# The first stage of a hybrid attention block: channel factors in 128-column steps on GpSimd, squares summed by halves and by TensorE, roots for two row tiles at a time

## The chip, the cores and the metric

The kernel runs on one core of one Trainium2 chip. The metric is the device time of one execution in microseconds (us), as the median of repeated runs. The engines are called by the letters of the profile: PE is TensorE (matmuls; PEld its weight loads), DVE is VectorE, ACT is ScalarE, POOL is GpSimd and SP is SyncE, which here only issues DMAs.

## The reference, cut to what matters

One block of a language model: a normalised projection, two mixers (a sparse attention and a gated linear attention), an output projection, and a convolutional feed-forward part. The change lies in the first two lines of the block alone, the normalisation and the part of the projection that makes the attention's keys and values, its gate logits and the low-rank gate input of the linear attention.

```python
def rms_norm(x, g):
    xf = x.astype(jnp.float32)
    y = xf * lax.rsqrt(jnp.mean(xf * xf, axis=-1, keepdims=True) + EPS)
    return (y * g.astype(jnp.float32)).astype(x.dtype)
...
    for l in range(DEPTH):
        z = rms_norm(h, attn_norm[l]) @ w_in[l]
        nq, nkv, ngate, gq, gk, gv, glr, gout = jnp.split(z, offs, axis=-1)
        o_nsa = nsa_mixer(...)
        o_gla = gla_mixer(...)
        h = h + jnp.concatenate([o_nsa, o_gla], axis=-1) @ w_out[l]
        u = causal_dwconv(rms_norm(h, ffn_norm[l]) @ w_up[l], conv_w[l], conv_b[l])
        gate, up = jnp.split(u, 2, axis=-1)
        h = h + (jax.nn.silu(gate) * up) @ w_down[l]
```

There are 1024 rows of 1024 channels, all in float32.

## The kernel before, in words

A float32 matrix product is made of three matmuls in the type fp32r: each operand is split into a high part (ACT copies it into fp32r, line L57) and a low part (an engine subtracts the high part from the original, line L60), and `zmm` adds high x high (L118), high x low weight (L119) and low x high weight (L120) for each of the 8 blocks k of 128 channels.

The first stage walks over 8 row tiles t of 128 rows. For each tile, `x_first` loads the transposed x as `xraw` (128 channels x 8 blocks k x 128 rows, 512 KB), squares it on ACT into `xsq` (L252), multiplies it in place by the channel factors `again` (L253: on DVE for t = 0, on POOL after that, one instruction of 1024 columns), and splits it in two halves `xt` (ACT L57, DVE L60). `x_stat` sums the squares over the 8 blocks k with one DVE reduction (L264, read with a stride), over the 128 partitions with a matmul against a column of ones (L265, written by the profile as two passes), and takes the inverse square root `rx` of that one column by twelve small DVE steps (`rsqrt`, L66 to L73 for one column; with more than one column the three Newton steps use the other form, L75 to L77).

The tile then goes through two products: with `WA` (296 columns: the inputs of the two compressions, and 40 columns of gates) and with `WC` (512 columns: selected and window keys and values). The row factor `rx` is applied when the results leave PSUM: two DVE instructions for WA (`kcvc` L289, `gl` L290), one on ACT (L201) and one on DVE (L204) for WC. `zp` gives two PSUM banks for these products, so a third product waits until one has been emptied. Then come norms and rotations of the keys, eight transposes (L220), and the split `xt` goes to memory (`x_d`, L294) for the later products. `x_first` and `x_stat` run two tiles ahead of the products.

The weights WA are loaded in four pairs of blocks k (`araw`, 303 KB each) and split with the low part on DVE and POOL in turn; the eight blocks of WC (`wraw`, four buffers) in the same way.

After the first stage come the two compressions, the query product, the attention with the linear attention woven into it (to about 600 us), and then the output projection and the feed-forward part. The order of the instructions on each engine is not the order of the program text: the framework's scheduler plans the whole kernel with a simulated timeline and a priority, and what it plans is fixed in the queue of each engine.

```python
    with tile.TileContext(nc, schedule_with_timeline_sim=True) as tc:
        body(tc, aps, o)
```

## Time and profile before

| what | value |
|---|---|
| median of 3 runs | 1359.92 us (1358.54 to 1360.41) |
| the profiled execution, its own time | 1360.02 us |
| span of the program in the profile | 1357.8 us |
| PE busy | 1311.7 us (97%) |
| PE weight loads busy | 1094.1 us (81%) |
| DVE busy | 1087.3 us (80%) |
| ACT busy | 701.8 us (52%) |
| POOL busy | 285.2 us (21%) |

The profiled execution took 2.2 us more than the span that its profile covers, which is the time before the first and after the last instruction. Busy shares are averages over the whole span. A matmul's duration in the trace includes the time in the pipeline, so that consecutive matmuls overlap; what a stream of them costs is read from the distance between their starts.

### The profile page before, as it was taken

To read this page: it belongs to the slowest core of one execution; us is meant where nothing else is said; L and a number is where in the kernel's file an instruction comes from. 1 tells how busy PE (TensorE), PEld (TensorE's weight loads), DVE (VectorE), ACT (ScalarE), POOL (GpSimd) and SP (SyncE) were. 2 spreads that over 40 slices of the span, in tenths; PEclk is the share of its full clock that TensorE was granted. 3 is DMA by queue.
4 is the path that set the end of the run, shared out by engine and by line. 5 is a ranking of instruction groups with operands and counts; after the bars stand their busy time and mean duration, and the time that the engine had idled before them with its cause. 6 is when DMAs were issued, how large, how long until landed. Compare 5 with 4: busy or idle time off the path is not lost.

```text
span 1357.8 us, 19773 instructions
## 1 busy us (share of the span) xinstructions
PE 1311.7 (97%) x6618; PEld 1094.1 (81%) x6618; DVE 1087.3 (80%) x2584; ACT 701.8 (52%) x1383; POOL 285.2 (21%) x437
## 2 busy tenths in 40 slices
PE   6899999999999998999999999999999998999998
PEld 5788788888888886768788888888888886888887
DVE  7996866788797869971688998888788878699774
ACT  5343666678665666663454544444444444444431
POOL 4222124549344455432500000000000000000000
PEclk9999999999999999999999999999999998999999
DMA  8537673325222224112742132222222229664173
GB/s 303 204 119 269 218 241 93 107 79 171 81 91 65 83 84 121 35 40 84 249 140 95 62 106 81 79 79 92 94 78 78 78 84 350 238 204 155 34 232 122
DMA packets 80535, 177.07 MB, mean 130 GB/s; under 512 B 10785, under 2 KB 22962, under 8 KB 80434
## 3 DMA queue, kind: packets, MB, share of 16 engines
q1 hardware_dynamic: 54450, 111.84, 24.7%
q0 software_dynamic: 10368, 37.75, 9.2%
q10 hardware_dynamic: 15616, 26.22, 5.3%
q8 instruction: 52, 0.85, 0.2%
q14 instruction: 49, 0.40, 0.1%
HBM read 133.84 MB, written 41.94 MB: 129 GB/s over the span
## 4 chain that ended last, share of the span: by engine, by line
PE 80%; DVE 12%; DMA 2%; issue 2%; ACT 2%; POOL 0%; SPq 0%; ACTq 0%; DVEq 0%; POOLq 0%
PE pda L982 9%; PE pdb L982 7%; PE z L118 4%; PE z L120 4%; PE z L119 4%; PE O L466 4%; PE S L448 4%; PE pt L459 3%; PE uZ L679 3%; PE uX L680 3%; PE uX L679 3%; PE uX L681 3%; PE uZ L680 3%; PE uZ L681 3%; PE uW L681 3%; PE uW L680 3%
## 5 line engine op out<-in xcount | busy, mean ns | idle before, releaser
L118 PE MATMUL z<-whi,xt 128*128 128x512 f32 (+1 forms) x384 | 141.7, 369 | 4.6 <-DVE rx L68 2.3
L119 PE MATMUL z<-wlo,xt 128*128 128x512 f32 (+1 forms) x384 | 140.3, 365 | 0.3 <-DVE wlo L60 0.2
L120 PE MATMUL z<-whi,xt 128*128 128x512 f32 (+1 forms) x384 | 139.8, 364 | 0.0
L60 DVE TENSOR_TENSOR PTl<-pt,PTh 128x512 fp32r<-128x512 f32 (+1 forms) x148 | 100.5, 684 | 35.1 <-ACT PTh L57 33.8
L453 ACT ACTIVATE P<-P,m 128x640 f32<-128x640 f32 (+7 forms) x128 | 94.0, 736 | 57.3 <-DVE m L450 55.0
L57 ACT ACTIVATE PTh<-pt 128x512 fp32r<-128x512 f32 (+1 forms) x148 | 86.2, 593 | 53.3 <-PE pt L459 44.8
L527 POOL TENSOR_SCALAR P<-P,sc 128x640 f32<-128x640 f32 (+7 forms) x128 | 89.6, 711 | 76.0 <-DVE sc L473 38.3
L448 PE MATMUL S<-kst,qst 128*128 128x320 f32 (+5 forms) x384 | 99.7, 352 | 4.1 <-DVE m L450 3.3
L57 ACT ACTIVATE wuh<-wuraw 128x512 fp32r<-128x512 f32 x65 | 40.6, 631 | 103.8 <-PE uZ L680 52.8
L459 PE MATMUL pt<-ident,P 128*128 128x128 f32 x528 | 85.4, 273 | 0.9 <-DVE PTl L60 0.8
L118 PEld LDWEIGHTS z<-whi,xt 128*128 128x128 f32 x384 | 73.7, 192 | 14.8 <-issue 2.5
L119 PEld LDWEIGHTS z<-wlo,xt 128*128 128x128 f32 x384 | 73.5, 191 | 10.3 <-DVE wlo L60 0.7
L120 PEld LDWEIGHTS z<-whi,xt 128*128 128x128 f32 x384 | 73.5, 191 | 10.1 <-issue 0.2
L57 ACT ACTIVATE wuh<-ws 128x512 fp32r<-128x512 f32 x76 | 47.6, 632 | 64.3 <-PE uW L680 30.1
L57 ACT ACTIVATE dh<-g 128x1024 fp32r<-128x1024 f32 x44 | 46.7, 1064 | 65.9 <-PE pdb L982 24.3
L459 PEld LDWEIGHTS pt<-ident,P 128*128 128x128 f32 x528 | 65.9, 140 | 15.5 <-PE S L448 1.4
L448 PEld LDWEIGHTS S<-kst,qst 128*128 128x128 f32 x384 | 63.4, 191 | 16.0 <-DVE m L450 9.3
L982 PE MATMUL pda<-dl,dh 128*128 128x512 f32 x176 | 68.3, 389 | 0.0
L982 PE MATMUL pda<-dh 128*128 128x512 f32 x176 | 68.3, 389 | 0.0
L982 PE MATMUL pda<-dh,dl 128*128 128x512 f32 x176 | 68.3, 389 | 0.0
L792 ACT ACTIVATE y<-u,cb,cw 128x1024 f32<-128x1024 f32 x44 | 54.4, 1240 | 20.3 <-DVE u L871 14.6
L466 PE MATMUL O<-PTl,Vst 128*128 128x512 f32 x132 | 58.6, 444 | 6.2 <-DVE PTl L60 6.0
(473 smaller groups left out, 3899.1 us busy)
## 6 DMA issues: line engine op xcount, KB each, us to landing
xt<-x_d POOLq DMA_DIRECT2D x48, 512.0 KB, 3.7
wuraw<-in_wU_dram SPq DMA_DIRECT2D x42, 512.0 KB, 3.7
dv<-in_wD_dram SPq DMA_DIRECT2D x55, 256.0 KB, 3.3
act_d<-y SPq DMA_DIRECT2D x22, 512.0 KB, 2.7
dv<-act_d SPq DMA_DIRECT2D x44, 256.0 KB, 3.5
x_d<-xt ACTq DMA_DIRECT2D x16, 512.0 KB, 4.7
xt<-mix_d POOLq DMA_DIRECT2D x16, 512.0 KB, 4.2
g<-in_wD_dram SPq DMA_DIRECT2D x22, 256.0 KB, 5.6
```

The costliest lines, as they stand in the source:

```text
L57: A.activation(dst, src, AF.Copy, scale=scale)
L60: (eng or V).tensor_sub(dst, src, hi.bitcast(F))
L118: T.matmul(ps, x[:, 0], wh, start=(k == 0), stop=False)
L119: T.matmul(ps, x[:, 0], wl, start=False, stop=False)
L120: T.matmul(ps, x[:, 1], wh, start=False, stop=(k == NK - 1))
L448: T.matmul(ps[:, :e - c], qst[:, h], kcols(i, c, e), start=(i == 0), stop=(i == 1))
L453: A.activation(Pt, Pt, AF.Exp, bias=m, scale=-1.0, accum_out=sc)
L459: T.transpose(tp[:n, h], get(h), ident)
L466: T.matmul(O, Vt, y[:n], start=(nmm[0] == 0), stop=(nmm[0] == total - 1))
L680: T.matmul(ps, wh[:, k], bl[:, k], start=False, stop=False, skip_group_check=True)
L681: T.matmul(ps, wl[:, k], bh[:, k], start=False, stop=(k == 3 and last), skip_group_check=True)
L982: T.matmul(ps[t], l[:, ts], r, start=(j == 0 and n == 0 and not add), stop=(j == NH - 1 and n == 2), skip_group_check=True)
```

## The change

`x_first` no longer squares. For tile 0 it loads x in two halves, with the first weight slices between them, and DVE multiplies each half by the factors; for the other tiles POOL does it in eight instructions, one for each block k, of 128 columns with the factor as a per-partition scalar. The product goes to a tile of its own, `xg` (one buffer). `x_stat` squares `xraw` in place on ACT, adds its halves twice on DVE (512 columns, then 256), and TensorE sums the two blocks that are left with two matmuls whose weights are the squares. Even and odd tiles share one PSUM tile, and the root is taken for two columns at once after the odd tile. The first four blocks of WA come one by one through the buffers of `wraw`, the other four in two pairs, and every low part of WA and WC is now made by DVE. Tile 1's x is loaded and its root taken ahead of the loads of WC. `kcvc` and `gl` become views of one tile `kg`, written by one instruction.

```diff
-        kcvc = cc.tile([128, NT, 256], F, name="kcvc")
-        gl = cc.tile([128, NT, 40], F, name="gl")
+        kg = cc.tile([128, NT, NA], F, name="kg")
+        kcvc, gl = kg[:, :, :256], kg[:, :, 256:]
...
-            def x_first(t, eng):
+            def x_first(t):
                 raw = xr_p.tile([128, NK, 128], F, name="xraw")
-                SY.dma_start(raw, I["xT"][t])
-                sq = xr_p.tile([128, NK, 128], F, name="xsq", bufs=1)
-                A.activation(sq, raw, AF.Square)
-                eng.tensor_tensor(raw, raw, again[:, :, None].to_broadcast([128, NK, 128]), op=OP.mult)
+                halves = [slice(4 * i, 4 * i + 4) for i in range(2)]
+                for i, ks in enumerate(halves if t == 0 else [slice(0, NK)]):
+                    SY.dma_start(raw[:, ks], I["xT"][t, :, ks])
+                    if t == 0:
+                        wa_load(2 * i)
+                        wa_load(2 * i + 1)
+                xg = xr_p.tile([128, NK, 128], F, name="xg", bufs=1)
                 xt = []
-                for i in range(2):
+                for i, ks in enumerate(halves):
+                    if t == 0:
+                        V.tensor_tensor(xg[:, ks], raw[:, ks], again[:, ks, None].to_broadcast([128, 4, 128]), op=OP.mult)
+                    else:
+                        for k in range(4 * i, 4 * i + 4):
+                            P.tensor_scalar(xg[:, k], raw[:, k], again[:, k:k + 1], 1.0, op0=OP.mult, op1=OP.mult)
                     x = (xfp if i else xtp).tile([128, 2, 4, 128], R, name="xt")
-                    split(x[:, 0], x[:, 1], raw[:, 4 * i:4 * i + 4], V)
+                    split(x[:, 0], x[:, 1], xg[:, ks], V)
                     xt.append(x)
-                return xt, sq
-
-            def x_stat(t, sq):
-                st = pp.tile([128, 512], F, name="st", tag="h1", bufs=2)
-                ssq = c2.tile([128, 128], F, name="ssq", tag="vv")
-                V.tensor_reduce(ssq, sq.rearrange("p k t -> p t k"), axis=X, op=OP.add)
-                T.matmul(st[:, 0:1], ssq, ones, start=True, stop=True)
-                rsqrt(c2, rx[:, t:t + 1], st[:, 0:1], 1.0 / D, 1)
...
+            def x_stat(t, raw, kept=[]):
+                if t % 2 == 0:
+                    kept.append(pp.tile([128, 512], F, name="st", tag="h1", bufs=2))
+                st, c = kept[-1], t % 2
+                A.activation(raw, raw, AF.Square)
+                for n in (4, 2):
+                    V.tensor_tensor(raw[:, 0:n], raw[:, 0:n], raw[:, n:2 * n], op=OP.add)
+                for k in range(2):
+                    T.matmul(st[:, c:c + 1], raw[:, k], ones, start=(k == 0), stop=(k == 1), skip_group_check=True)
+                if c:
+                    rsqrt(c2, rx[:, t - 1:t + 1], st[:, 0:2], 1.0 / D, 2)
...
+            def wa_load(k):
+                if k < 4:
+                    wa_raw[k] = rawp.tile([128, 512], F, name="wraw")[:, :NA]
+                    SY.dma_start(wa_raw[k], I["wA"][k // 2, :, k % 2])
+                else:
+                    wa_raw[k] = wap.tile([128, 2, NA], F, name="araw", bufs=2)
+                    SY.dma_start(wa_raw[k], I["wA"][k // 2])
+            SY.dma_start(again, I["again"])
+            xts[0], sq = x_first(0)
+            for k in (0, 1, 2, 3, 4, 6):
+                if k > 3:
+                    wa_load(k)
+                    split(wah[:, k:k + 2], wal[:, k:k + 2], wa_raw[k], V)
+                else:
+                    split(wah[:, k], wal[:, k], wa_raw[k], V)
             x_stat(0, sq)
-            WC = [w_load(I["wC"][1, k], 512, V if k % 2 else P) for k in range(NK)]
+            xts[1], sq = x_first(1)
+            x_stat(1, sq)
+            WC = [w_load(I["wC"][1, k], 512, V) for k in range(NK)]
...
-            xts[1], sq = x_first(1, P)
-            x_stat(1, sq)
...
-                V.tensor_scalar(kcvc[:, t], ps[:, :256], rx[:, t:t + 1], None, op0=OP.mult)
-                V.tensor_scalar(gl[:, t], ps[:, 256:NA], rx[:, t:t + 1], None, op0=OP.mult)
+                V.tensor_scalar(kg[:, t], ps[:, :NA], rx[:, t:t + 1], None, op0=OP.mult)
```

## Rows read from the trace of the kernel before

**Rows 1.** Windows, 0-104 us: length; PE, PEld, DVE, ACT, POOL busy; PEclk; DMA share; GB/s.
```profile
0.00:10.00 10.00, 0.38 (x1) 0.38 (x2) 3.39 (x4) 5.62 (x9) 2.12 (x6) 1.00 0.83 280
10.00:30.00 20.00, 18.28 (x86) 15.10 (x86) 19.32 (x46) 9.41 (x17) 12.04 (x8) 1.00 0.92 324
30.00:60.00 30.00, 25.66 (x131) 21.83 (x129) 29.71 (x82) 13.95 (x26) 10.34 (x11) 0.94 0.60 211
60.00:104.00 44.00, 43.73 (x254) 38.43 (x254) 40.88 (x133) 18.64 (x37) 8.67 (x19) 1.00 0.43 143
```

**Rows 2.** Groups of PE by form, 0 to 60 us: count, busy us, mean ns, idle.
```profile
L118 PE MATMUL z<-whi,xt 128*128 128x512 f32 x32 | 13.9, 435 | 4.3 <-DVE rx L68 2.3 <-DVE rs_u L72 2.0
L118 PE MATMUL z<-wah,xt 128*128 128x296 f32 x34 | 11.1, 326 | 9.6 <-ACT xt L57 9.6
```

**Rows 3.** Timeline of PE, 14 to 52 us: start us, duration us, instruction.
```profile
14.16 0.45 PE L119 MATMUL z<-wal,xt 128*128 128x296 f32 x1
...
19.12 0.39 PE L120 MATMUL z<-whi,xt 128*128 128x512 f32 x1
19.35 0.30 PE L119 MATMUL z<-wal,xt 128*128 128x296 f32 x1
19.48 0.30 PE L120 MATMUL z<-wah,xt 128*128 128x296 f32 x1
...
20.17 0.28 PE L265 MATMUL st<-ones,ssq 128*128 128x1 f32 x2
...
51.62 0.50 PE L118 MATMUL z<-whi,xt 128*128 128x512 f32 x1 [2.30 <-DVE rx L68]
```

**Rows 4.** Timeline of all engines, the first 10 us.
```profile
0.75 0.38 SPq L270 DMA_DIRECT2D araw<-in_wA_dram  x1
...
3.68 0.70 ACT L57 ACTIVATE wah<-araw 128x592 fp32r<-128x592 f32 x1 [1.65 <-DMA araw<-in_wA_dram]
...
6.36 1.06 ACT L252 ACTIVATE xsq<-xraw 128x1024 f32<-128x1024 f32 x1 [1.98 <-DMA xraw<-in_xT_dram]
...
9.62 0.61 PE L118 MATMUL z<-wah,xt 128*128 128x296 f32 x1 [9.62 <-ACT xt L57]
```

**Rows 5.** Groups of DVE by form, 0 to 130 us.
```profile
L264 DVE TENSOR_REDUCE ssq<-xsq 128x128 f32<-128x1024 f32 x8 | 16.1, 2014 | 0.0
L60 DVE TENSOR_TENSOR xt<-xraw,xt 128x512 fp32r<-128x512 f32 x16 | 14.3, 905 | 0.0
...
L72 DVE TENSOR_SCALAR rs_u<-rs_u,rs_a 128x1 f32<-128x1 f32 x25 | 5.3, 210 | 0.3
...
L290 DVE TENSOR_SCALAR gl<-z,rx 128x40 f32<-128x40 f32 x8 | 2.0, 250 | 0.0
...
L76 DVE TENSOR_TENSOR rs_u<-rs_u,rs_a 128x8 f32<-128x8 f32 x12 | 1.9, 162 | 0.2
```

**Rows 6.** Timelines of DVE and of POOL, places where they run side by side.
```profile
11.69 2.76 DVE L60 TENSOR_TENSOR xt<-xraw,xt 128x512 fp32r<-128x512 f32 x2
12.88 1.04 POOL L305 TENSOR_SCALAR hgain<-hgain 128x512 f32<-128x512 f32 x1
...
24.14 0.68 DVE L60 TENSOR_TENSOR wlo<-wraw,whi 128x512 fp32r<-128x512 f32 x1
24.35 2.23 POOL L253 TENSOR_TENSOR xraw<-xraw,again 128x1024 f32<-128x1024 f32 x1 [0.18 <-ACT xsq L252]
25.48 0.21 DVE L72 TENSOR_SCALAR rs_u<-rs_u,rs_a 128x1 f32<-128x1 f32 x1
...
48.39 2.07 POOL L253 TENSOR_TENSOR xraw<-xraw,again 128x1024 f32<-128x1024 f32 x1
48.70 2.31 DVE L60 TENSOR_TENSOR xt<-xraw,xt 128x512 fp32r<-128x512 f32 x1
```

**Rows 7.** Groups of POOL by form, whole span.
```profile
L253 POOL TENSOR_TENSOR xraw<-xraw,again 128x1024 f32<-128x1024 f32 x7 | 13.8, 1971 | 25.4 <-ACT xsq L252 21.1 <-DVE rs_u L72 4.3
...
L527 POOL TENSOR_SCALAR P<-P,sc 128x128 f32<-128x128 f32 x16 | 5.9, 380 | 1.5 <-DVE sc L473 0.9 <-DVE ro L77 0.5
```

More of the change, by code (lines that the diff above doesn't have):

```diff
@@ L268, in body @@
-            for k2 in range(4):
-                raw = wap.tile([128, 2, NA], F, name="araw", bufs=2)
-                SY.dma_start(raw, I["wA"][k2])
-                ks = slice(2 * k2, 2 * k2 + 2)
-                if k2 == 0:
-                    SY.dma_start(again, I["again"])
-                    xts[0], sq = x_first(0, V)
-                split(wah[:, ks], wal[:, ks], raw, P if k2 % 2 else V)
+                return xt, raw
+            def x_stat(t, raw, kept=[]):
[9 more added lines that the diff above has]
+                    rsqrt(c2, rx[:, t - 1:t + 1], st[:, 0:2], 1.0 / D, 2)
@@ new lines, in body @@
+            wa_raw = {}
+            def wa_load(k):
[13 more added lines that the diff above has]
+                    split(wah[:, k], wal[:, k], wa_raw[k], V)
@@ L276, in body @@
             x_stat(0, sq)
-            WC = [w_load(I["wC"][1, k], 512, V if k % 2 else P) for k in range(NK)]
+            xts[1], sq = x_first(1)
+            x_stat(1, sq)
+            WC = [w_load(I["wC"][1, k], 512, V) for k in range(NK)]
             for dst, name in ((ident, "ident"), (rope, "rope"), (hgain, "hgain")):
                 SY.dma_start(dst, I[name])
-            xts[1], sq = x_first(1, P)
-            x_stat(1, sq)
             for t in range(NT):
                 if t + 2 < NT:
-                    xts[t + 2], sq = x_first(t + 2, P)
+                    xts[t + 2], sq = x_first(t + 2)
```

## The prediction, made before the changed kernel was run

> **What bounds the kernel now.** I read the page first: PE is busy nearly all the way, and the two slices of it that stand out are the first two, some 68 us, which is where the change lies. So I read the windows of that stretch next. In them the reader is to see two different regimes [rows 1]. From 60 to 104 us PE is busy 43.73 of 44.00 us and DVE 40.88: PE is the bound. From 10 to 60 us DVE is busy 49.03 of 50 us, PE has holes, and in the first 10 us PE does one matmul.
>
> How much PE loses there I work out from counts and distances between starts, because durations overlap. A 512-column matmul takes 0.23 us from start to start (19.12 to 19.35), a 296-column one 0.13 (19.35 to 19.48), which I take as 0.137, since the starts are rounded [rows 3]. By 60 us PE had issued 32 of the 512-column matmuls on L118, as many on L119 and L120, and 34 of the 296-column ones, 34 and 33 on the two other lines [rows 2]: 96 x 0.23 + 101 x 0.137 = 35.9 us. Some twenty short ones (transposes, sums) add about 1.6. So 37.5 of 60 us were work, and **22.5 us were lost**. From 60 to 104 us I take 0.8 us lost, an estimate of the same kind from the 0.27 us that PE is not busy there and the short distances. What PE does not lose here comes off the end of the kernel, since PE has no slack later on (97% over the span).
>
> The lost time has three parts. The first matmul starts at 9.62 us, because x lands at 6.36 and is squared, multiplied and split one after the other, with the 303 KB of weights ahead of it in the queue [rows 4]. Then PE runs slowly after its idle start: a 296-column matmul lasts 0.45 us at 14 us and 0.30 at 19 us [rows 3], as at the lower of its clock's two levels (1.2 and 2.4 GHz). The granted clock of the windows reads 1.00 there and 0.94 from 30 to 60 us [rows 1], so for the start I go by the durations. And from 10 to 60 us DVE feeds PE too slowly: at 51.62 PE had waited 2.30 us for a product bank to be emptied [rows 3], and what held DVE was one subtraction of 512 columns that lasted 2.31 us beside a POOL multiplication from 48.39 to 50.46; one of the same size takes 0.68 us at 24.14 [rows 6].
>
> **The change part by part.** On DVE:
>
> - The reduction goes, 2.01 us a tile [rows 5]. Two additions replace it: 0.68 us for 512 columns by the subtraction of the same size [rows 6], and half of that, 0.34. Saved 0.99 x 8 = 7.9 us.
> - The roots: eight of twelve steps each, nine of them at 0.21 and three that I put at 0.16, are 19.0 us; four of twelve steps at 0.16, the price of the eight-column form, are 7.7 [rows 5]. Saved 11.3.
> - One instruction for `kg` saves 0.25 us a tile less the 40 columns, some 0.04: 1.7 in all [rows 5].
> - All low parts of the weights now come to DVE: four of 512 columns at 0.68 and two pairs of 592 at 0.77 by proportion. Added 4.3.
>
> That is 16.6 us less DVE work in a stretch in which DVE was busy 93.3 of 104 us [rows 1]. The waits behind POOL come on top. The 16 subtractions for x average 0.905 us against 0.68, so 3.6 us in this group alone [rows 5, 6].
>
> On POOL the multiplication of 1.97 us becomes eight steps; the nearest row is a scaling of 128 columns at 0.38 us, so 3.0 us a tile, 1.1 more [rows 7]. POOL was busy 33 of 104 us [rows 1], and it loses the six weight subtractions, so this is hidden; if x were late for it, the cost would be 1.1 us for each of 7 tiles.
>
> On ACT the square moves behind the multiplication. It takes the same 1.06 us, and ACT is busy less than half the time [rows 1, 4]: nothing. On PE there are 16 more passes of one column. Two of them last 0.28 us [rows 3]; with half of it overlapped, as with the other matmuls, eight more pairs add **1.1 us**, and 2.2 if nothing overlaps. On SP the loads ahead of WC become nine issues instead of six at 0.38 us [rows 4], and tile 1's x goes ahead of WC too, 512 KB at 324 GB/s, or 1.6 us [rows 1]. Both ends of that: WC's last block 2.7 us later, or nothing, because DVE and not the transfer sets WC's pace (below). I take nothing.
>
> The **start**. The 303 KB issued at 0.75 were in use at 3.68, 2.9 us later [rows 4]. Half of x is issued at about 1.2 us, so it lands at about 4.1; DVE multiplies it in 0.68, ACT rounds it in about 0.6, and the first matmul starts at **5.4 us** instead of 9.62. Until tile 0 has passed both products, DVE sets the pace. Its work up to there, in durations: x of tile 0 and 1 multiplied, where DVE does it, and subtracted (4.1), WA (4 x 0.4 + 2 x 0.77 = 3.1), additions (2.0), one root (1.9), WC (5.4), `kg` (0.5): 17 us, and some 14 by start-to-start distance, from 4.1 us on. So WC is complete between 18 and 21 us; I take 20. By then PE has done tile 0 (24 x 0.23 + 24 x 0.137 = 8.8 us) and about 2 us of tile 1, whose product has a bank once the first root has come: **9.2 us lost** by 20 us, 7 at best and 13 at worst.
>
> **After that** DVE needs 2.6 us less per tile than before (7.9 + 11.3 + 1.7 over 8 tiles) and is no longer saturated. PE lost about 7 us between 30 and 60. Left over: some waits behind POOL. I take **2.5 us**, from 0.5 (as from 60 to 104 us) to 7 (all as before).
>
> How a GpSimd step holds DVE. The subtraction at 48.70 ended only after POOL's 1024-column instruction had, while a one-column step at 25.48 ran in 0.21 us beside another [rows 6]. And the two subtractions from 11.69 took 2.76 us together while POOL's next instruction, begun at 12.88, took 1.04: they took turns, and neither was starved [rows 6]. So the wait is for the rest of one instruction, and one of 0.38 us can hold DVE for 0.38 at most, where 1.97 held it for 1.6. The Trainium skill, SBUF — State Buffer, section "Who interferes with whom", says that a DVE instruction with two SBUF inputs waits for a whole GpSimd instruction that reads SBUF, that one with a single such input does not, and that a reduction never does; by that rule, with which these rows agree, the change is worth less than the count of instructions says (1349.5 by the count, 1354 to 1358 by the rule taken at its strictest), because it turns reductions and one-column steps, which never wait, into additions and two-input steps, which can.
>
> **The sum.** Lost before 22.5 + 0.8 = 23.3 us; after 9.2 + 2.5 + 1.1 = 12.8; difference 10.5. The profiled execution took 1360.02 us, 0.1 above the median of the runs, so 1360.0 - 10.5 = **1349.5 us**.
>
> **The rivals.**
>
> 1. The waits behind POOL stay. Some 20 two-input DVE instructions a tile meet POOL steps that fill 3.0 of 10 us; each then waits 0.2 on average: 20 x 0.3 x 0.2 = 1.2 us a tile, more than the 0.5 that the x subtractions wait now. Then DVE is near saturation again, PE keeps its holes after 20 us (7 lost instead of 2.5), and the start comes out between my 9.2 and its worst end of 13: 23.3 - 13 - 7 - 1.1 = 2.2 to 23.3 - 9.2 - 7 - 1.1 = 6 us gained, 1354 to 1358. For it: a tile's multiplication takes POOL longer. Against it: 16.6 us of plain work are gone whatever the waits do.
> 2. The gain is given back later. The scheduler plans the order anew from other times, in the attention too, where PE shares the bound with DVE. No row prices this. From the 0.8 us that PE loses in 44 us of well-fed work I allow 3 us either way; for no change at all it would have to take 8 or more: within 2.7 us of 1360.
> 3. Slower: the sums of squares come late. Their matmuls stand in PE's queue, and now hang on POOL's eight steps, then ACT's square, two additions. If DVE takes a turn between every two steps, the steps last 8 x (0.38 + 0.68) = 8.5 us instead of 3.0. Where the plan leaves no room for it, PE waits up to 5.5 us for each of 7 tiles. This decides from 1.5 us a tile, 10.5 in all; at 2.5 the time is 1367. Against it: x is prepared two tiles ahead, some 18 us of PE's work, and DVE has fewer such instructions than would be needed.
>
> **How the numbers follow.** The sum as it stands (a gain of 8 to 14 us): 0.58, with a range of its own of 1346 to 1352. Rival 1: 0.20. A gain above 14, when the start is at its best end and the later order falls well: 0.07. Rival 2 without any gain: 0.08. Rival 3: 0.07. The range that holds eight in ten: 1343.5 to 1357. Faster by over 0.2% (2.7 us, about what a measurement tells from no change): 0.85; within: 0.08; slower: 0.07.
>
> **What would show each step.** The first matmul at 5 to 6 us; DVE busy well under 9.5 of 10 us between 20 and 60; the WC product of tile 0 emptied near 20 us; subtractions for x near 0.7 us on average; no PE wait of 2 us behind a root, and no granted clock under 1.00 from 30 to 60 us. PE reaches the end of tile 7 some 10 us earlier, and that distance is unchanged at 600 us. The prediction is wrong if PE waits for the sums (L265's place), if the first root comes after 20 us so that both banks stand full, or if the distance shrinks in the attention.

## The result, and the profile after

The changed kernel takes **1369.12 us** (median of five runs, 1364.11 to 1370.06); the kernel before, run beside it, 1358.92 (1357.86 to 1360.41). The ratio is 1.0066 [1.005, 1.0082]: slower by two thirds of a per cent, where 1349.5 was predicted. The profiled execution has a span of 1366.7 us against 1357.8, so 8.9 us more.

The windows answer to [rows 1] (the same columns: length; PE, PEld, DVE, ACT, POOL busy; PEclk; DMA share; GB/s), changed kernel:

```profile
0.00:10.00 10.00, 3.37 (x10) 2.49 (x10) 4.42 (x9) 4.83 (x8) 0.20 (x4) 1.00 0.71 223
10.00:30.00 20.00, 16.30 (x56) 12.80 (x56) 12.67 (x28) 10.28 (x17) 8.14 (x17) 0.93 0.93 340
30.00:60.00 30.00, 24.29 (x121) 20.96 (x121) 20.39 (x57) 11.64 (x21) 12.27 (x26) 0.90 0.60 202
60.00:104.00 44.00, 44.00 (x257) 39.21 (x257) 32.04 (x115) 17.19 (x33) 15.73 (x38) 0.99 0.30 108
```

DVE was to be relieved, and it was: busy 69.5 of 104 us instead of 93.3. Part of that difference is work that only came later; up to the end of the stage (108.2 and 99.6 us, as defined below) DVE was busy 73.4 us instead of 89.2, 15.8 less. But PE did not use it. By 60 us it had issued 187 matmuls where the kernel before had issued 218, although it began four microseconds earlier. The time that DVE no longer works became idle time of DVE.

The groups by form, changed kernel: PE from 0 to 60 us ([rows 2]), DVE from 0 to 130 us ([rows 5]), and POOL's multiplication over the span ([rows 7]).

```profile
L118 PE MATMUL z<-wah,xt 128*128 128x296 f32 x30 | 12.6, 419 | 12.2 <-ACT xt L57 5.6 <-DVE kg L313 4.6 <-DVE vv L204 1.5
L118 PE MATMUL z<-whi,xt 128*128 128x512 f32 x24 | 10.6, 449 | 1.1 <-ACT whi L57 1.1
```
```profile
L60 DVE TENSOR_TENSOR xt<-xg,xt 128x512 fp32r<-128x512 f32 x16 | 11.7, 731 | 9.7 <-ACT xt L57 9.6
L276 DVE TENSOR_TENSOR xraw<-xraw 128x512 f32<-128x512 f32 x8 | 5.6, 702 | 3.9 <-ACT xraw L274 3.7
L313 DVE TENSOR_SCALAR kg<-z,rx 128x296 f32<-128x296 f32 x8 | 4.2, 524 | 4.6 <-PE z L120 4.6
L76 DVE TENSOR_TENSOR rs_u<-rs_u,rs_a 128x2 f32<-128x2 f32 x12 | 2.2, 184 | 0.2
```
```profile
L263 POOL TENSOR_SCALAR xg<-xraw,again 128x128 f32<-128x128 f32 x56 | 26.3, 489 | 45.8 <-DMA xraw<-in_xT_dram 16.3 <-DVE wal L60 11.3 <-DVE xt L60 10.0
```

The subtractions for x fell from 905 to 731 ns, so the long locks beside POOL are nearly gone. The last entries of a line tell what is new: PE stood 4.6 us behind `kg`, that is, behind WA's result that had not yet left its bank, and DVE itself now stands 9.6 us behind ACT's `xt` and 3.7 behind the square.

**Where PE stands still.** PE's timeline of the changed kernel ([rows 3]), then DVE's:

```profile
23.57 0.47 PE L120 MATMUL z<-whi,xt 128*128 128x512 f32 x1
25.99 0.41 PE L118 MATMUL z<-wah,xt 128*128 128x296 f32 x1 [1.96 <-DVE kg L313]
...
52.62 0.58 PE L278 MATMUL st<-ones,xraw 128*128 128x1 f32 x4 [1.49 <-DVE rs_a L66]
55.88 0.61 PE L118 MATMUL z<-wah,xt 128*128 128x296 f32 x1 [2.68 <-DVE kg L313]
56.29 0.45 PE L119 MATMUL z<-wal,xt 128*128 128x296 f32 x1
```
```profile
21.90 0.16 DVE L66 TENSOR_SCALAR rs_a<-st 128x2 f32<-128x2 f32 x1 [0.84 <-PE st L278]
...
22.61 0.30 DVE L75 SCALAR_TENSOR_TENSOR rs_u<-rx 128x2 f32<-128x2 f32 x1
...
25.41 0.53 DVE L313 TENSOR_SCALAR kg<-z,rx 128x296 f32<-128x296 f32 x1
...
51.33 1.15 DVE L276 TENSOR_TENSOR xraw<-xraw 128x512 f32<-128x512 f32 x2 [1.36 <-ACT xraw L274]
52.40 0.15 DVE L66 TENSOR_SCALAR rs_a<-st 128x2 f32<-128x2 f32 x1
...
53.54 0.16 DVE L75 SCALAR_TENSOR_TENSOR rs_u<-rx 128x2 f32<-128x2 f32 x1
...
55.30 0.53 DVE L313 TENSOR_SCALAR kg<-z,rx 128x296 f32<-128x296 f32 x1
```

Both PE waits end with a root for two tiles followed by `kg`: the root begins at 21.90 and at 52.40, `kg` is written from 25.41 and from 55.30 on, and PE goes on 0.58 us after either. After the second wait PE also comes back at the lower level of its clock: 296-column matmuls last 0.45 us where they last 0.30 at the upper one [rows 3].

Tile 2 shows what the sharing does. Its sum is on PE at 37.40, its root is taken with tile 3's at 52.40. What stands between is read from the chain of waits of the changed kernel, and below it one row of ACT's timeline:

```profile
37.40 0.35 PE st L278 x4
37.80 3.47 DMA xraw<-in_xT_dram
41.27 0.75 POOL xg L263 x3
...
46.38 3.83 POOL xg L263 x8
50.24 1.07 ACT xraw L274
51.33 0.70 DVE xraw L276
...
55.38 0.45 DVE kg L313
```
```profile
39.75 0.63 ACT L57 ACTIVATE xt<-xg 128x512 fp32r<-128x512 f32 x1 [0.66 <-PE z L120]
```

POOL multiplies tile 3 from 41.27 and tile 4 from 46.38 (the tile `xg` has one buffer, so they follow one another). The DMA of the chain, from 37.80, is not what tile 3 waited for: it is tile 4's load and landed at 41.99, and tile 3's x had landed at 27.0. What tile 3 waited for is `xg`: tile 2's second half left it only with ACT's rounding from 39.75, which waited for a matmul of PE (L120), that is, for a buffer of `xt`, and with DVE's subtraction, which ended at 41.17. Tile 4's additions, behind its square on ACT, then stand ahead of the root on DVE. So tile 2's results wait in their bank for the whole preparation of tile 3, and, by the order of DVE's queue, for that of tile 4 as well. The first WC results left PSUM 12 us later than before, as the summary of ACT's scaling of them (count, min/median/max ns, first and last start) shows, first the kernel before, then the changed one, both from 15 to 60 us:

```profile
L201 ACT ACTIVATE zqk<-z,rx x4: 456/460/474, 28.3 to 59.6; 128x256 f32<-128x256 f32 x4
```
```profile
L201 ACT ACTIVATE zqk<-z,rx x3: 456/464/473, 40.3 to 55.3; 128x256 f32<-128x256 f32 x3
```

Only some 4 of these 12 us go with the shared root: with a root for each tile (e1 below) the first one starts at 36.4 us, and with WC's buffers left to WC as well (e6 below) at 29.3. The rest belongs to the start.

**The start.** The first matmul of the changed kernel begins at 5.64 us (before: 9.62 [rows 4]), and yet as much was lost by 20 us as before. PE's timeline and SyncE's of the changed kernel, and below them SyncE's of the kernel before:

```profile
5.64 0.62 PE L118 MATMUL z<-wah,xt 128*128 128x296 f32 x1 [5.64 <-ACT xt L57]
...
15.39 0.63 PE L118 MATMUL z<-whi,xt 128*128 128x512 f32 x1
...
18.34 0.80 PE L118 MATMUL z<-whi,xt 128*128 128x512 f32 x1 [1.06 <-ACT whi L57]
```
```profile
18.03 2.78 SPq L101 DMA_DIRECT2D wraw<-in_wC_dram  x3
21.93 0.33 SPq L252 DMA_DIRECT2D xraw<-in_xT_dram  x1
22.36 0.38 SPq L101 DMA_DIRECT2D wraw<-in_wC_dram  x1
```
```profile
11.80 3.68 SPq L101 DMA_DIRECT2D wraw<-in_wC_dram  x4
```

Tile 0's 24 matmuls with WA take from 5.64 to 15.39, at the slow pace and with waits for slices of WA. The second four blocks of WC are issued from 18.03 to 22.36 us, where the kernel before issued them from 11.80 to 15.5: the four `wraw` buffers first hold slices of WA, and are freed by DVE's subtractions. In the first 10 us 223 GB/s moved instead of 280. Of the 15.7 us that are lost by 20 us (the measure is explained below), 5.6 lie before the first matmul. Some 3.6 are the slow pace: all 29 product matmuls up to 20 us last as at the lower level of the clock (0.45 us for 296 columns, 0.63 for 512, where [rows 3] has 0.30 and 0.39). The rest, some 6, are waits for slices of WA and blocks of WC and the slower first matmuls behind them. In the kernel before the three parts are 9.6, 2.5 and 2.6 us.

### The profile page after: what moved, and what is told of

It is laid out like the page before. It is cut to its first block, busy times and chain, and to the rows that moved or that the text cites. A ratio compares the mean times of both kernels' runs of the same rounds, so it can differ in the third digit from the quotient of the medians.

```text
span 1366.7 us, 19815 instructions
## 1 busy us (share of the span) xinstructions
PE 1320.4 (97%) x6634; PEld 1101.1 (81%) x6634; DVE 1071.2 (78%) x2545; ACT 702.5 (51%) x1385; POOL 289.5 (21%) x480
## 4 chain that ended last, share of the span: by engine, by line
PE 80%; DVE 11%; DMA 4%; issue 2%; ACT 2%; POOL 1%; SPq 1%; ACTq 0%; DVEq 0%; POOLq 0%
PE pda L1005 9%; PE pdb L1005 7%; PE z L118 5%; PE z L120 4%; PE z L119 4%; PE O L489 4%; PE S L471 4%; PE pt L482 3%; PE uZ L702 3%; PE uX L703 3%; PE uX L702 3%; PE uX L704 3%; PE uZ L703 3%; PE uZ L704 3%; PE uW L702 3%; PE uW L704 3%
## 5 line engine op out<-in xcount | busy, mean ns | idle before, releaser
L118 PE MATMUL z<-whi,xt 128*128 128x512 f32 (+1 forms) x384 | 141.6, 369 | 1.1 <-ACT whi L57 1.1
L120 PE MATMUL z<-whi,xt 128*128 128x512 f32 (+1 forms) x384 | 139.6, 364 | 0.0
L550 POOL TENSOR_SCALAR P<-P,sc 128x640 f32<-128x640 f32 (+7 forms) x128 | 89.2, 707 | 75.9 <-DVE sc L496 37.9
L118 PEld LDWEIGHTS z<-whi,xt 128*128 128x128 f32 x384 | 73.4, 191 | 11.2 <-ACT whi L57 1.8
L120 PEld LDWEIGHTS z<-whi,xt 128*128 128x128 f32 x384 | 73.4, 191 | 9.9 <-issue 0.2
L482 PEld LDWEIGHTS pt<-ident,P 128*128 128x128 f32 x528 | 65.9, 140 | 15.5 <-PE S L471 1.5
L815 ACT ACTIVATE y<-u,cb,cw 128x1024 f32<-128x1024 f32 x44 | 54.3, 1239 | 20.3 <-DVE u L894 14.7
```

The costliest lines, as they stand in the source:

```text
L118: T.matmul(ps, x[:, 0], wh, start=(k == 0), stop=False)
L120: T.matmul(ps, x[:, 1], wh, start=False, stop=(k == NK - 1))
L482: T.transpose(tp[:n, h], get(h), ident)
```

## The experiments

To see where PE loses time I took, over all matmuls of a trace, the distance to the next start less what it is at the upper clock for that many columns [rows 3], and added up what was above it, with the time before the first. The kernel before loses 23.0 us in this way by 60 us (the prediction had 22.5). "Stage" is the start of the 128th matmul of L118, of which the eight tiles' products have 128. Each ratio is against runs of the kernel before on the same chip, whose median was 1358.9 us for the changed kernel and 1360.3 to 1361.4 for the others, so that differences between rows are good to some 2 us. The last four columns come from one execution each; in e2 and e4 it took 2.2 and 3.2 us more than the median, in e5, e7, e14 and e16 2.1 to 3.4 less.

| kernel | median us | ratio [95%] | lost 0-20 | 20-60 | 60-100 | stage us |
|---|---|---|---|---|---|---|
| before | 1360.6 | | 14.7 | 8.3 | 1.5 | 99.6 |
| changed | 1369.1 | 1.0066 [1.005, 1.0082] | 15.7 | 15.7 | 2.5 | 108.2 |
| e1 root per tile | 1360.0 | 0.9999 [0.9988, 1.001] | 15.2 | 6.7 | 3.1 | 98.8 |
| e2 square first | 1361.4 | 1.0011 [1.0, 1.0022] | 14.5 | 9.1 | 2.9 | 100.5 |
| e3 tile 1 after WC | 1369.6 | 1.0068 [1.0043, 1.0094] | 14.1 | 15.7 | 2.1 | 106.2 |
| e4 parts on before | 1363.8 | 1.0029 [1.0017, 1.0042] | 16.2 | 5.6 | 5.5 | 101.2 |
| e5 shared root on before | 1365.4 | 1.003 [1.0015, 1.0046] | 14.6 | 8.6 | 5.1 | 102.7 |
| e6 e1, WA in pairs | 1358.8 | 0.9982 [0.9964, 1.0] | 14.8 | 4.8 | 1.7 | 95.1 |
| e7 e1, one POOL step | 1360.5 | 0.9996 [0.998, 1.0012] | 15.7 | 4.4 | 3.1 | 97.1 |
| e8 e1 and e2 | 1365.2 | 1.0028 [1.0016, 1.0041] | 14.4 | 8.2 | 3.6 | 100.2 |
| e9 third bank | 1372.6 | 1.0082 [1.0062, 1.0102] | 12.6 | 13.3 | 2.0 | 101.5 |
| e10 third bank, before | 1368.5 | 1.0054 [1.0035, 1.0072] | 14.1 | 1.2 | 2.1 | 90.9 |
| e11 e6, one POOL step | 1359.7 | 0.9993 [0.9983, 1.0003] | 15.4 | 5.3 | 2.7 | 97.2 |
| e12 e6, WC lows shared | 1361.1 | 1.0006 [0.9991, 1.0021] | 15.5 | 5.9 | 2.8 | 97.9 |
| e13 other bank, before | 1357.0 | 0.9969 [0.9957, 0.9981] | 14.2 | 2.1 | 2.8 | 93.3 |
| e14 other bank, changed | 1361.1 | 1.0005 [0.9993, 1.0016] | 14.5 | 5.5 | 3.1 | 96.8 |
| e15 e6, other bank | 1356.5 | 0.9967 [0.9956, 0.9978] | 12.3 | 3.6 | 2.0 | 91.8 |
| e16 sums' bank, before | 1366.6 | 1.004 [1.0026, 1.0053] | 16.9 | 7.3 | 6.7 | 106.4 |
| e17 e6, sums' bank | 1376.3 | 1.0117 [1.0102, 1.0132] | 14.6 | 12.4 | 10.3 | 110.6 |

The theories, by the letters of the expectations: **A**, the shared root holds the even tile's banks; **B**, the sums come late because square and additions stand behind POOL's steps; **C**, tile 1's x goes ahead of WC; **D**, the scheduler's new order moves the time by several us, whatever the edit. **E**, which comes in late, is about the loss behind the first stage in e13: that it comes from the bank taken from the compressions.

### One part of the change undone: e1, e2, e3

e1, a sum's tile and a root for each row tile:

```diff
-                if t % 2 == 0:
-                    kept.append(pp.tile([128, 512], F, name="st", tag="h1", bufs=2))
-                st, c = kept[-1], t % 2
+                st, c = pp.tile([128, 512], F, name="st", tag="h1", bufs=2), 0
...
-                if c:
-                    rsqrt(c2, rx[:, t - 1:t + 1], st[:, 0:2], 1.0 / D, 2)
+                rsqrt(c2, rx[:, t:t + 1], st[:, c:c + 1], 1.0 / D, 1)
```

> The changed kernel with one part undone: each row tile has its own PSUM column and takes its own root, with the one-column steps, as before the change. Theory A (the shared root holds the even tile's product until the odd tile's squares are summed): both long waits of PE for the emptied bank, 2.0 us at 26 us and 2.7 us at 56 us, go, with the slow clock behind each; 1358 to 1362 us. Theory B (the one buffer of the factored x makes tile 3 wait until tile 0's second product is done, whoever takes the root): the wait at 26 us goes, but tile 3 is still late and PE waits for it some us later; 1364 to 1367. Theory C (the loss comes from the loads and weight splits of the first 25 us): no more than 2 us better, 1366 to 1369.

1360.0 us. This one edit takes back the whole loss, 9.1 us. DVE is busy 80.15 of 104 us, 10.6 more than in the changed kernel, in part because the stage runs ahead of it. Its two windows from 10 to 60 us:

```profile
10.00:30.00 20.00, 18.46 (x71) 14.67 (x70) 15.29 (x45) 9.71 (x16) 8.52 (x17) 1.00 0.95 347
30.00:60.00 30.00, 28.34 (x160) 24.78 (x159) 22.20 (x86) 14.00 (x25) 14.18 (x32) 1.00 0.61 220
```

The granted clock is back at 1.00, and no PE wait behind `kg` is left (the longest from 10 to 104 us is 1.7 us behind a root). From 20 to 60 us 6.7 us are lost instead of 15.7.

e2, the square taken first and into the second tile, so that it does not wait for POOL (from tile 1 on), the shared root kept:

```diff
+                sq = raw if t == 0 else xg
+                if t:
+                    A.activation(sq, raw, AF.Square)
+                    xg = raw
...
-                A.activation(raw, raw, AF.Square)
+                if t == 0:
+                    A.activation(raw, raw, AF.Square)
```

> The changed kernel with one part undone: from tile 1 on ACT squares the raw x into the second tile at once, and GpSimd's eight steps multiply in place, so that the sum of squares no longer stands behind the multiplication and its one buffer; roots still for two tiles. Theory A: the shared root still ties tile 0 to tile 1, but tile 1's sum comes 4 us earlier (GpSimd's eight steps took 4.4 us ahead of the square), so the wait at 26 us shrinks to nothing and that at 56 us too; 1360 to 1363. Theory B: tile 3 is squared and multiplied as soon as it has landed; the wait at 56 us goes; 1361 to 1364. Theory C: 1366 to 1369.

1361.4. That fits A and B alike: with the odd tile's sum early, sharing a root costs next to nothing, so here the price is that of two things together, a bank that waits for the other tile and a long way to that tile's sum.

e3, tile 1's load and root behind WC's loads, as before the change:

```diff
-            xts[1], sq = x_first(1)
-            x_stat(1, sq)
             WC = [w_load(I["wC"][1, k], 512, V) for k in range(NK)]
             for dst, name in ((ident, "ident"), (rope, "rope"), (hgain, "hgain")):
                 SY.dma_start(dst, I[name])
+            xts[1], sq = x_first(1)
+            x_stat(1, sq)
```

> The changed kernel with the load, split and sum of tile 1 moved back behind the loads of the second weights, where they stood before the change. Theory C: the first four blocks of the second weights are requested some 2 us earlier, are split without standing behind tile 1 on DVE, and tile 0's second product is ready near 30 us instead of 39; 1360 to 1364. Theory A: the root of tiles 0 and 1 comes later still, the product bank of tile 0 is held longer, PE stands still for 5 us more; 1372 to 1378.

1369.6, no better than the changed kernel: C is out as the main cause. A had said worse; it stayed equal. PE waits 4.4 us for a sum (L278, behind DVE's addition), and the granted clock from 10 to 30 us falls to 0.72:

```profile
10.00:30.00 20.00, 14.27 (x46) 8.98 (x45) 11.97 (x21) 8.93 (x16) 10.14 (x17) 0.72 0.93 315
```

### Parts of the change on the kernel before: e4, e5

e4 adds to the kernel before POOL's 128-column steps (in place), the sums by halves with two matmuls, and `kg`; loads, roots and order of the text stay:

```diff
+                    for k in range(NK):
+                        P.tensor_scalar(raw[:, k], raw[:, k], again[:, k:k + 1], 1.0, op0=OP.mult, op1=OP.mult)
...
-                V.tensor_reduce(ssq, sq.rearrange("p k t -> p t k"), axis=X, op=OP.add)
-                T.matmul(st[:, 0:1], ssq, ones, start=True, stop=True)
+                for n in (4, 2):
+                    V.tensor_tensor(sq[:, 0:n], sq[:, 0:n], sq[:, n:2 * n], op=OP.add)
+                for k in range(2):
+                    T.matmul(st[:, 0:1], sq[:, k], ones, start=(k == 0), stop=(k == 1))
```

> The kernel before with three parts of the change alone: GpSimd's multiplication in eight steps of 128 columns (in place, after the square), squares summed by halves and by two matmuls, and one instruction for the 296 columns; loads, weight splits, order of the text and one root per tile as before. All theories agree that these parts are sound: GpSimd no longer holds DVE for 2 us, DVE has 9.6 us less to do, PE's waits of 2.2 and 2.3 us at 38 and 51 us go. 1350 to 1354. If the plan of the scheduler decides by chance (theory D: any change of the text moves the time by some us), it lies anywhere from 1352 to 1366.

A miss: 1363.8. DVE is busy 78.6 of 104 us, and PE gains 2.7 us from 20 to 60, but it loses 4 more from 60 to 100, and more behind the stage (below, with e8). One load of x lands late between 60 and 100; ACT's timeline and PE's waits (10 to 104 us: total, times, longest):

```profile
66.44 1.06 ACT L252 ACTIVATE xsq<-xraw 128x1024 f32<-128x1024 f32 x1 [3.98 <-DMA xraw<-in_xT_dram]
```
```profile
PE trk L220 <- ACT comb L57: 3.2, 1, 3.2
PE st L270 <- DVE xsq L268: 2.6, 2, 2.1
```

e5 shares the root on the kernel before, and nothing else:

```diff
+                if t % 2 == 0:
+                    kept.append(pp.tile([128, 512], F, name="st", tag="h1", bufs=2))
+                st, c = kept[-1], t % 2
...
-                rsqrt(c2, rx[:, t:t + 1], st[:, 0:1], 1.0 / D, 1)
+                if c:
+                    rsqrt(c2, rx[:, t - 1:t + 1], st[:, 0:2], 1.0 / D, 2)
```

> The kernel before with the shared root alone: sums of squares as before the change, but the root of an even tile is taken with that of the odd one. Theory A1 (the shared root costs by itself, because the even tile's product waits for a tile that is loaded one step later): PE waits for emptied banks at the even tiles; 1364 to 1370 us. Theory A2 (it costs only where the odd tile's sum stands behind the multiplication and its one buffer): the square follows the landing at once here, the root of the odd tile is there in time except at the start, where tile 1 is loaded at 7.8 us; 1358 to 1363.

1365.4 by the median (the profiled execution, 1361.99, is at the low end). The shared root by itself is a loss, of 4 to 5 us here and 9 in the changed kernel. The wait that A gives as its reason is not in this trace: from 20 to 60 us no more is lost than before (8.6 beside 8.3), no PE wait stands behind a root, and those behind `kcvc` and `vv`, which empty the banks, come to 0.7 and 0.6 us. So e5 shows a price, and not what it is paid for.

### What is left of the change with a root for each tile: e6, e7, e8, e11, e12

All begin from e1. e6 loads WA in four pairs through `araw`, so that `wraw` belongs to WC alone; e7 makes POOL's multiplication one instruction of 1024 columns; e8 adds e2's edit; e11 is e6 with e7's edit; e12 is e6 with WC's low parts on POOL and DVE in turn.

The edits of e6, then of e7 and e11, then of e12:

```diff
-                        wa_load(2 * i + 1)
...
-                if k < 4:
-                    wa_raw[k] = rawp.tile([128, 512], F, name="wraw")[:, :NA]
...
-            for k in (0, 1, 2, 3, 4, 6):
+            for k in (0, 2, 4, 6):
```
```diff
-                            P.tensor_scalar(xg[:, k], raw[:, k], again[:, k:k + 1], 1.0, op0=OP.mult, op1=OP.mult)
+                        if i == 0:
+                            P.tensor_tensor(xg, raw, again[:, :, None].to_broadcast([128, NK, 128]), op=OP.mult)
```
```diff
-            WC = [w_load(I["wC"][1, k], 512, V) for k in range(NK)]
+            WC = [w_load(I["wC"][1, k], 512, V if k % 2 else P) for k in range(NK)]
```

> The changed kernel with a root per tile (1360.0 us), and with the first weights in pairs of blocks through their own two buffers, as before, instead of single blocks through the buffers of the second weights. Theory C1 (what the earlier start gains, 4 us at the first matmul, is lost because the second weights get their four buffers late, at 6 to 10 us instead of 3 to 5): the second weights are requested some 2 us earlier, tile 0 is done earlier; 1356 to 1358. Theory C2 (the start is held by the transfer itself and by DVE's order, not by these buffers): 1359 to 1362.

> The changed kernel with a root per tile (1360.0 us), and GpSimd's multiplication as one instruction of 1024 columns into the second tile, instead of eight steps. If the long GpSimd instruction holding DVE was worth what the trace of before suggests (a wait of 2.3 us on PE with slow matmuls behind it, seven times at risk): 1363 to 1367. If DVE now has so much idle time that it catches up: 1359 to 1362.

> The changed kernel with both repairs: a root per tile (alone 1360.0 us) and the square ahead of GpSimd's in-place multiplication (alone 1361.4). If they repair one and the same coupling, the second adds nothing: 1359 to 1361. If each has a wait of its own, 1355 to 1358.

> The changed kernel with a root for each tile, WA in four pairs through its own two buffers, and POOL's multiplication as one instruction of 1024 columns: what is left of the change is the early first half of x, the product in a tile of its own, the sums by halves, kg and the low parts on DVE. Theory A: the two repairs measured 1360.0 and 1358.8 us and the one step 1360.5 beside 1360.0, so 1357 to 1360 us, a little faster than before. Theory D (the order is planned anew and moves the time by several us either way, so repairs don't add up): anything from 1356 to 1365.

> The changed kernel with a root for each tile, WA in pairs, and WC's low parts made by POOL and DVE in turn as before the change. DVE gets 2.7 us less work ahead of tile 0's second product, POOL four instructions of 512 columns more, at about 1.0 us each. If DVE's plain work set the pace of the start, WC is complete 2 to 3 us earlier and the time is 1355 to 1357 us. If it is the loads of WC, which wait for the four buffers, nothing changes: 1357.5 to 1360.5 us, and as much is lost by 20 us as in the kernel with DVE alone (14.8 us).

e6: 1358.8, and the stage ends 4.5 us earlier than before; at the end of the kernel some 2 us of that are left. e7 (1360.5) and e11 (1359.7) show that the 128-column steps are worth nothing measurable, and e12 (1361.1) that sharing WC's low parts brings nothing: 15.5 us are lost by 20 us all the same.

e8 (1365.2) is a miss: each repair alone brings the time back to that of before, both together cost 4 to 5 us, so that with the square first a root for each tile is 2 to 4 us dearer than a shared one. Its stage is not to blame. At the end of it e8 is 0.6 us behind the kernel before, and 5.7 at the compression's transposes of `ch` (139.5 us in the kernel before). Between them DVE stands for a rounded weight block of the next product (`whi`), the compression's additions (`tb`) stand behind that in DVE's queue, and PE waits for these. First e8 (a row of DVE's timeline, PE's waits from 95 to 150 us, a window), then the kernel before:

```profile
102.83 0.69 DVE L60 TENSOR_TENSOR wlo<-wraw,whi 128x512 fp32r<-128x512 f32 x1 [3.00 <-ACT whi L57]
...
PE h L355 <- DVE tb L351: 3.5, 1, 3.5
...
115.00:120.00 5.00, 5.00 (x14) 3.96 (x14) 3.43 (x13) 1.26 (x3) 2.17 (x7) 0.54 0.76 278
```
```profile
PE h L330 <- DVE tb L326: 1.3, 1, 1.3
...
115.00:120.00 5.00, 5.00 (x25) 4.24 (x24) 2.09 (x8) 2.93 (x4) 0.46 (x2) 1.00 0.88 296
```

Behind the longer wait the granted clock is 0.54 instead of 1.00, and PE issues 14 matmuls instead of 25. The same pair of waits, DVE's for `whi` and PE's for `tb`, is 2.50 and 3.1 us in e4, 2.40 and 2.9 in e12, 2.06 and 2.5 in e6, but 1.19 and 1.7 in e2 and 1.05 and 1.6 in e1. So an order that is no worse in the stage can lose in the step behind it, which is what D says and no other theory here; why that weight block comes late in some orders the runs do not show.

### A third bank for the products: e9, e10, e13 to e17

All kernels so far share two product banks. e9 and e10 give the changed kernel and the one before a third one and take one of three from the key transposes; e13, e14 and e15 leave those alone, and let WA's product use the bank `tr` of the compressions, on the kernel before, the changed one and e6; e16 and e17 use the sums' banks `h1` instead, on the kernel before and on e6.

The edits of e9 and e10, then of e13 to e15, then of e16 and e17:

```diff
-TK = 3
+TK = 2
-        zp = pool(sp, "zpC", 2, PSUM)
+        zp = pool(sp, "zpC", 3, PSUM)
```
```diff
-                ps = zp.tile([128, 512], F, name="z")
+                ps = pp.tile([128, 512], F, name="z", tag="tr", bufs=TC)
```
```diff
-                ps = zp.tile([128, 512], F, name="z")
+                ps = pp.tile([128, 512], F, name="z", tag="h1", bufs=2)
```

> The changed kernel with a third PSUM bank for the two products (and one bank less, two in place of three, for the transposes of the keys); the shared root stays. Theory A (the shared root costs the time because the even tile's product stands in one of two banks until the odd tile's root has come): PE can start one more product meanwhile, 2.2 us for one of 24 matmuls of 296 columns or 5.5 us for one of 512, at each of the four roots, so most of the 9 us goes: 1360 to 1364 us, and the waits of L118 behind kg (4.6 us) nearly vanish. Theory B (it is not the bank, but that x itself comes late, since its buffers are held): the third bank changes nothing, 1367 to 1370 us, and L118 waits behind xt instead. One bank less for the transposes may cost something; the next kernel tells how much.

> The kernel before with the same exchange of a bank, as a control. There every tile has a root of its own and the waits of L118 behind the root came to some 4 us in the first 60 us. Theory A, as far as a bank counts here too: 1356 to 1360 us. If the missing transpose bank costs anything it shows here: 1361 us or more.

e10 is the most telling of all runs, though it is slower. Its windows from 10 to 60 us, beside which [rows 1] are to be laid:

```profile
10.00:30.00 20.00, 18.88 (x92) 16.50 (x93) 18.33 (x42) 10.53 (x18) 12.81 (x9) 1.00 0.95 346
30.00:60.00 30.00, 29.97 (x169) 26.10 (x168) 28.90 (x85) 13.52 (x27) 7.19 (x11) 1.00 0.65 240
```

DVE is as busy as in the kernel before (18.33 and 28.90 us), with the same instructions, and PE issues 169 matmuls from 30 to 60 us instead of 131: 1.2 us are lost from 20 to 60 instead of 8.3. So DVE's busy share was not what held PE there; two banks were. A relieved DVE empties two banks sooner, and that too is worth something from 20 to 60 us: with two banks 5.6 are lost in e4, where no PE wait behind the root [rows 2] is left, and 4.4 in e7, of the 8.3. The stage ends at 90.9, 8.7 us earlier. It loses this again later, with PE waits of 3.8 us in the compression, 2.6 for a product (behind `qk`) and 2.2 for a transpose's bank (`trk` behind `qst`), of which there is one less; but e14, which has all three, shows the same 2.2. On the changed kernel (e9) the stage gains 6.7 us and the wait behind `kg` falls from 4.6 to 1.9, so A holds, but the time does not fall (1.0082 beside 1.0066, within their intervals), which I had not expected.

> The kernel before, with WA's product of each tile in the PSUM bank that is idle through the first stage, so that three banks serve the products and nothing is taken from the transposes. Theory A (two banks held PE from 20 to 60 us, DVE's busy share did not): the last L118 matmul of the first stage starts at about 91 us instead of 99.6, PE loses under 2 us from 20 to 60 us with DVE as busy as before, and the time is 1350 to 1353 us. Theory D (the planned order gives back elsewhere what the banks bring): 1356 to 1362 us, with the first stage shorter all the same.

> The changed kernel with the same idle bank for WA's products; the shared root stays. Theory A: the waits behind kg vanish as with the exchanged bank, the last L118 of the first stage starts at about 101 us instead of 108, and the time is 1361 to 1364 us, still above the same edit on the kernel before, since the shared root also delays the tiles whose buffers hang on it. Theory D: 1366 to 1373 us.

> The changed kernel with a root for each tile, WA in pairs through its own buffers, and the idle bank for WA's products. If the relief of DVE is worth something once a bank is free for every product, this is faster than the kernel before with the idle bank alone: PE loses 15 us by 20 us as in all kernels, under 2 from 20 to 60, and the time is 1348 to 1352 us. If the relief is worth nothing it equals that kernel within 2 us. Theory D: 1354 to 1362 us.

e13: 1357.0, with the stage at 93.3 and 2.1 us lost from 20 to 60, DVE again at its limit (its window, and then those from 104 to 160 us of e13 and of the kernel before):

```profile
30.00:60.00 30.00, 29.32 (x166) 25.55 (x165) 29.65 (x86) 13.89 (x27) 9.61 (x11) 1.00 0.63 223
...
104.00:160.00 56.00, 51.00 (x230) 40.85 (x231) 34.37 (x126) 20.60 (x31) 9.79 (x25) 0.91 0.54 178
```
```profile
104.00:160.00 56.00, 54.73 (x273) 44.74 (x272) 41.41 (x145) 24.13 (x38) 11.55 (x28) 1.00 0.69 236
```

6.3 us are gained by the stage's end and 3.6 are left at the end of the kernel; from 104 to 160 us PE is busy 3.7 us less than before. The bank was not idle, as I had called it: the compression's first transposes (L316) go into it from 23.1 us on in the kernel before, and only from 98.1 in e13.

e14: 1361.1, so one more bank takes 8.0 us off the changed kernel and 3.6 off the one before: the banks are worth more where the root is shared. e15: 1356.5, within 0.4 of e13. Where a third bank serves the products, the kernel is no faster with all of DVE's relief than without it. These two, e13 and e15, are the only kernels clearly faster than before, and what makes them so is not in the change.

> The kernel before, with WA's products in the two PSUM banks that the sums of squares use (each sum leaves its bank within 3 us), nothing else. Theory E (the loss between 100 and 160 us came from the bank of the compression's transposes): the first stage ends at about 92 us as with the other banks, the compression's transposes start near 23 us again, and the time is 1350 to 1355 us. Theory D (the order gives it back anyway): 1356 to 1360 us. If a sum's bank comes free too late for the next product, PE waits at L118 or L265 and the first stage ends later than 96 us.

> The changed kernel with a root for each tile and WA in pairs through its own buffers, and the sums' banks for WA's products. Theory E: 1349 to 1354 us. If the relief of DVE is worth nothing, equal within 2 us to the kernel before with the same banks; if it counts once PE is held by nothing else, 3 us or more faster than that. Theory D: 1355 to 1360 us.

Both miss, on the side that the first expectation names last: 1366.6 and 1376.3. A sum now shares its bank with a product. In e16 PE waits at the sums (L265, five times), by the profile for DVE's reduction, and the stage ends later than in the kernel before:

```profile
PE st L265 <- DVE ssq L264: 6.5, 5, 3.1
```

The edit costs 5 us here and 17.5 on e6. That this is a loss of the shared root's kind, a tile held by another through a bank, I only argue: in e17 PE's waits at the sums come to 0.8 us, and 13.8 are for blocks of WC, most of them before its first matmul. Whether the loss after the stage in e13 comes from its bank these two cannot say, since their stage was never short.

## Why the prediction was wrong

In the prediction's own measure 12.8 us were to be lost; 33.9 were (15.7 by 20 us, 18.2 from 20 to 100). Some 6.5 of these 21 lie in the start, the rest behind it.

**The roots were costed as DVE work only.** "four of twelve steps at 0.16 ... Saved 11.3": the saving on DVE is real, but a root for two columns after the odd tile makes the even tile's results wait, and this wait had no term in the sum. e1 puts it at 9 us in this kernel, and e14 confirms the bank: the shared root with one more bank is at 1361.1. e5 has the shared root at 4 to 5 us in the kernel before, without showing this wait. The prediction had even named its sign ("if the first root comes after 20 so that both banks stand full") among what would make it wrong, without pricing it; the first root came at 21.90 and the next at 52.40.

**"From 10 to 60 us DVE feeds PE too slowly" took a busy share for the cause.** 16.6 us less work were to be 4.5 us less lost after 20 us. DVE lost 15.8 us of busy time by the end of the stage, and e10 and e13 show PE running nearly without a hole beside the unrelieved DVE, once three products fit. With two banks and a root for each tile the relief does bring 1.6 to 3.9 of the 4.5 (e1, e6, e7), because DVE empties the banks sooner; with a third one it brings nothing (e15). The 2.30 us wait at 51.62 [rows 3] was what it said, a wait for a bank. I went past the bank to the engine that was to empty it, and past that to the POOL instruction beside it.

**The start.** 9.2 us lost by 20 us were predicted, 15.7 measured, 13 being my worst end; no kernel came below 12.3. The first matmul was right (5.4, measured 5.64). What failed is "DVE sets the pace ... WC is complete between 18 and 21 us": the last block of WC was issued at 22.36 us, for want of a buffer. That term I had at nothing, 2.7 us at most; from the second issues' 15.5 to 22.7 it is 7. But the buffers alone did not make the loss: e6 gives them back and still loses 14.8 us by 20 us (and 1.9 less than e1 from 20 to 60). The sum also left out that PE's early matmuls run at the lower level of its clock, which the prediction had read in the kernel before. At the distances from start to start seen there, 0.25 us for 296 columns and 0.43 for 512, the 48 matmuls of tile 0 take some 16 us and not 8.8, an estimate for the lower level all the way; in the changed kernel it lasted to 23 us.

**Rival 3** gave 1367 and was nearest by its number, but that is luck: it came through PE's wait at the sums, of which 1.5 us are there. Its slack, "x is prepared two tiles ahead, some 18 us", did not hold: tile 3 was multiplied only from 41.27 us, since `xg` has one buffer, which tile 2 held until PE had freed a buffer of `xt`. Whether a second one helps was not tried.

**Right were** the shorter subtractions (0.73 us, "near 0.7"), `kg` and the additions, POOL's longer way (3.75 us a tile; 3.0 was predicted), and that the difference made in the stage stays: 8.6 us at its end, 9.7 at 600 us, 8.9 over the span. Rival 1's waits behind POOL hardly exist.

**What stays open.** Edits that shorten the stage lose a part of it again. In the profiled executions e6 has 4.5 us at the end of the stage and 1.5 over the span, e13 6.3 and 3.0, e15 7.8 and 3.1; only e7 keeps its 2.5 (3.0 over the span, in an execution 3.3 us below the median). Part of it goes in the wait for `tb`, as in e8 and e4. That the order planned anew gives back the rest, and why, is argued from windows and waits, not shown by an experiment.

## What to carry to other kernels

A step that serves two tiles at once saves its instructions and makes the first tile wait for the second: before counting the saving, ask what the first tile holds in the meantime (here one of two PSUM banks), and follow the second one's way through its load, its buffers and the queues. A busy share near one shows an engine with much to do, not that it alone holds another; give the other one more buffer and see, since that costs one line.

## What the hardware showed that was not expected

POOL and DVE take turns between steps, and either can pay. The summary of POOL's 128-column steps in the changed kernel (min/median/max ns) and of DVE's two-column step:

```profile
L263 POOL TENSOR_SCALAR xg<-xraw,again x56: 362/372/1322, 11.8 to 84.4; 128x128 f32<-128x128 f32 x56
```
```profile
L75 DVE SCALAR_TENSOR_TENSOR rs_u<-rx x12: 154/161/314, 22.6 to 93.3; 128x2 f32<-128x2 f32 x12
```

While eight POOL steps ran from 22.18 us in 2.80 us, undisturbed, the root's steps beside them took 0.30 us (22.61) where they take 0.16 alone (53.54): the first shared root, from 21.90 to `kg` at 25.41 with the banks full, lasted some 1 us longer by it. Other POOL steps took up to 1.32 us. The Trainium skill, SBUF — State Buffer, section "Who interferes with whom", says that a DVE instruction with two SBUF inputs contends with a GpSimd instruction that reads SBUF. The doubled steps agree with it (0.30 against 0.16 us). For an instruction with one input the section makes an exception of DVE's two-port modes, which the prediction left out when it said that such a one does not wait: the two-column step with one input at 22.30 (L68) took 0.28 us beside POOL and 0.17 alone (53.33), while the one-column steps of e1 took as long beside POOL as alone (0.20 to 0.22 us). But all this is not what made the holes in PE: with a root for each tile the same POOL steps cost nothing (e1, 1360.0 us, beside e7, 1360.5).
